# Feed-forward up projections by Strassen's scheme, hidden rows through DRAM, in a two-block kernel

## The chip, the cores and the metric

The kernel runs on one core of a Trainium2 chip. A core has TensorE (PE, matrix products), VectorE (DVE), ScalarE (ACT), GpSimd (POOL), and SyncE (SP), whose queue issues the DMAs. The metric is device time in microseconds (us) of one execution; the median of three runs is given.

## The reference, cut to what matters

Two blocks follow each other on x of 1024 tokens by 1024 features (float32). Each ends its layer with a feed-forward part on a normalised h; the first has 4096 hidden features, the second 2816 of them, made from 2 times 2816 columns through a depthwise convolution over tokens (3 taps).

```python
# first block
h = rmsnorm(x, g_ffn[i])
x = x + jnp.square(jax.nn.relu(h @ w_ffn_up[i])) @ w_ffn_down[i]
...
# second block
h = rms_norm(x, g_ffn[l])
up = depthwise_conv(h @ w_up[l], conv_f_w[l], conv_f_b[l], FFN_CONV // 2)
act = jax.nn.gelu(up[..., :D_FF_2], approximate=True) * up[..., D_FF_2:]
x = x + act @ w_down[l]
```

## The kernel before

Every product is made of three matmuls of a 128x128 weight by 128x512 operand, since each operand is kept as a high and a low part: high by high (L89), high by low (L90), low by high (L91), in `mm3`. `split` (L58, L59) makes the two parts: ScalarE casts the high one, VectorE subtracts it for the low one. `load_w` brings 512 KB of weights in one DMA (`wraw`) and splits them into `whi` and `wlo`, 128x1024 each.

Activations stand transposed, features on partitions, tokens along the row, in two halves of 512 tokens: h0 (high `h0h`, low `h0l`) and h1. An up tile f (128 hidden features) takes, for each half, 8 parts of the inner dimension by 3 matmuls: 48 matmuls and one load of weights. The results are evacuated from PSUM and split into `hh` and `hl` in a ring of 5 pairs (pool "hid"). First feed-forward (`phase_ffn1`): ScalarE relu (L1098), VectorE square (L1099), split. Second (`phase_ffn2`): tiles f and f+22 belong together; each goes through ScalarE (L1487) and two scalar_tensor_tensor on VectorE (L1488, L1489, the outer taps), then gelu (L1495, ScalarE), product (L1496, VectorE), split.

Up and down are interleaved: `ffn` makes the tiles of one group (4, at the start fewer) and one more, then `tm` multiplies the group by its rows of the down weights for all tokens, and `add_x` (L1046, VectorE) adds each PSUM tile into the resident `xres`. A framework sets one static order for each engine and places the waits on semaphores. Before the feed-forward, `norm_rest` starts the up products on the first half of the tokens while the second half is still normalised and transposed (L232, `tr`, TensorE). There are 8 tiles of 128 tokens; `nst` holds their norms, whose small steps are on GpSimd (L194, L196).

Of the kernel before, what the change touches and what calls it, by code (L numbers as in the profile page):

```python
# [27 lines left out]
class Kern:  # L28
# [1035 lines left out]
    def ffn(self, st, nf, up, w_down, last=2, gain=None):  # L1064

        dp = self.pool(st, "hid")
        hid = {}
# [18 lines left out]
        self.behind = ()  # L1086

    def phase_ffn1(self):
        nc, A = self.nc, self.A
        with ExitStack() as st:  # L1090
            self.pp = self.pool(st, "psD", space=PSUM)
            self.mmb = 3
            h = self.norm_rest()

            def up(f, hi, lo):
                def ev(_, ps):
# [483 lines left out]
```

## Time and profile before

| | |
|---|---|
| runs, median (lowest to highest) | 3458.9 us (3456.75 to 3462.65) |
| the profiled execution | 3458.02 us, of which the span of the profile is 3456.0 |
| TensorE busy | 3363.2 us, 97% of the span |
| VectorE, ScalarE, GpSimd busy | 1642.6, 1193.1, 262.6 us |
| mean granted clock of TensorE | 0.994 of full speed |

Busy time is the share of the span in which an engine has an instruction in work. A matmul's busy time overlaps that of the next one (each is shown as about 0.39 us long), so how fast TensorE goes is read from the distance of two starts. The first feed-forward lies at about 1113 to 1790 us and the second at about 2700 to 3456 us of the span.

### The profile page before, as it was taken

The numbers are of one execution on the slowest core, as the hardware profiler recorded it, in microseconds if no ns is written. First come the engines' busy times: TensorE is split into PE (matmuls) and PEld (weight loads), VectorE is DVE, ScalarE is ACT, GpSimd is POOL, SyncE is SP. The second block draws the span as 40 slices with busy tenths as digits, with TensorE's granted clock in tenths as the row PEclk, the third lists the DMA queues.
The fourth block names the chain that finished last, engine by engine and source line by source line (L and its number), as shares of the span: only waits on it lengthen the run. The fifth ranks groups of instructions, "written<-read, shape, count | busy, mean of one in ns | idle before, by whom it ended". The sixth has DMA issues, their size and how long they took to land.

```text
span 3456.0 us, 45568 instructions
## 1 busy us (share of the span) xinstructions
PE 3363.2 (97%) x18990; PEld 2769.9 (80%) x18990; DVE 1642.6 (48%) x2475; ACT 1193.1 (35%) x1624; POOL 262.6 (8%) x448
## 2 busy tenths in 40 slices
PE   8999999999989999999999999999999999999998
PEld 8867777777778888888889977778779888888887
DVE  4445666466554333333343566756343543434434
ACT  4343443477422211111122476652121321211212
POOL 0101111122100000000001411110000000000000
PEclk9999999999999999999999999999999999999999
DMA  3532232332371111111112212222553111211211
GB/s 119 170 107 72 75 78 63 92 85 71 124 274 50 37 49 49 49 49 49 49 55 68 89 56 73 69 75 73 159 188 122 51 49 31 62 48 37 61 49 55
DMA packets 332395, 274.80 MB, mean 80 GB/s; under 512 B 85934, under 2 KB 278814, under 8 KB 332190
## 3 DMA queue, kind: packets, MB, share of 16 engines
q1 hardware_dynamic: 332190, 271.90, 25.6%
q8 instruction: 149, 2.44, 0.3%
q14 instruction: 56, 0.46, 0.0%
HBM read 209.97 MB, written 61.88 MB: 79 GB/s over the span
## 4 chain that ended last, share of the span: by engine, by line
PE 83%; DVE 8%; ACT 5%; issue 2%; DMA 1%; POOL 1%; SPq 0%; DVEq 0%; ACTq 0%; POOLq 0%
PE mm L90 24%; PE mm L89 24%; PE mm L91 24%; PE rps L797 1%; PE tr L232 1%; PE lr L89 1%; PE tp L501 1%; PE rps L713 1%; DVE sq L1301 1%; PE lr L90 1%; DVE hs L1315 1%; PE lr L91 1%; DVE th L1318 1%; DVE ri L1313 1%; DVE wlo L59 1%
## 5 line engine op out<-in xcount | busy, mean ns | idle before, releaser
L58 ACT CAST whi<-wraw 128x1024 fp32r<-128x1024 f32 (+4 forms) x272 | 273.6, 1008 | 1229.7 <-PE mm L90 641.4
L59 DVE TENSOR_TENSOR wlo<-wraw,whi 128x1024 fp32r<-128x1024 f32 (+4 forms) x272 | 318.8, 1176 | 733.8 <-ACT whi L58 728.5
L89 PE MATMUL mm<-h0h,whi 128*128 128x512 f32 x1040 | 405.0, 391 | 6.2 <-ACT h0h L58 2.3
L91 PE MATMUL mm<-h0h,wlo 128*128 128x512 f32 x1040 | 405.6, 390 | 0.0
L90 PE MATMUL mm<-h0l,whi 128*128 128x512 f32 x1040 | 405.1, 390 | 0.1
L90 PE MATMUL mm<-h1l,whi 128*128 128x512 f32 x944 | 368.0, 390 | 0.0
L91 PE MATMUL mm<-h1h,wlo 128*128 128x512 f32 x944 | 367.7, 389 | 0.0
L89 PE MATMUL mm<-h1h,whi 128*128 128x512 f32 x944 | 367.3, 390 | 0.0
L89 PE MATMUL mm<-whi,hh 128*128 128x512 f32 x864 | 339.3, 393 | 1.0 <-DVE cv L1489 0.7
L90 PE MATMUL mm<-wlo,hh 128*128 128x512 f32 x864 | 340.3, 394 | 0.0
L91 PE MATMUL mm<-whi,hl 128*128 128x512 f32 x864 | 335.2, 389 | 0.0
L1046 DVE TENSOR_TENSOR xres<-mm,xres 128x512 f32<-128x512 f32 (+1 forms) x272 | 166.2, 654 | 311.4 <-PE mm L91 311.4
L89 PEld LDWEIGHTS mm<-h0h,whi 128*128 128x128 f32 x1040 | 195.3, 188 | 48.8 <-ACT h0h L58 3.1
L90 PEld LDWEIGHTS mm<-h0l,whi 128*128 128x128 f32 x1040 | 195.5, 188 | 41.2 <-DVE h0l L59 0.6
L91 PEld LDWEIGHTS mm<-h0h,wlo 128*128 128x128 f32 x1040 | 195.6, 188 | 40.8
L89 PEld LDWEIGHTS mm<-h1h,whi 128*128 128x128 f32 x944 | 177.0, 188 | 37.8 <-ACT h1h L58 0.7
L90 PEld LDWEIGHTS mm<-h1l,whi 128*128 128x128 f32 x944 | 177.3, 188 | 37.0
L91 PEld LDWEIGHTS mm<-h1h,wlo 128*128 128x128 f32 x944 | 177.1, 188 | 37.0
L89 PEld LDWEIGHTS mm<-whi,hh 128*128 128x128 f32 x864 | 162.2, 188 | 39.8 <-issue 1.2
L91 PEld LDWEIGHTS mm<-whi,hl 128*128 128x128 f32 x864 | 162.2, 188 | 36.3 <-DVE hl L59 0.3
L90 PEld LDWEIGHTS mm<-wlo,hh 128*128 128x128 f32 x864 | 162.4, 188 | 32.4
L194 POOL TENSOR_SCALAR nst<-nst 128x2 f32<-128x2 f32 (+1 forms) x41 | 10.0, 243 | 2079.1 <-ACT hn L212 1352.8
(477 smaller groups left out, 6357.6 us busy)
## 6 DMA issues: line engine op xcount, KB each, us to landing
wraw<-in_w_in_dram SPq DMA_DIRECT2D x66, 512.0 KB
wraw<-in_w_up_dram SPq DMA_DIRECT2D x44, 512.0 KB
wraw<-in_w_ffn_up_dram SPq DMA_DIRECT2D x32, 512.0 KB
wraw<-in_w_ffn_down_dram SPq DMA_DIRECT2D x32, 512.0 KB
g<-gate_d SPq DMA_DIRECT2D x24, 512.0 KB
wraw<-in_w_down_dram SPq DMA_DIRECT2D x22, 512.0 KB
gate_d<-zg SPq DMA_DIRECT2D x32, 256.0 KB
wraw<-in_w_out_dram SPq DMA_DIRECT2D x16, 512.0 KB
```

The costliest lines, as they stand in the source:

```text
L58: return (self.nc.scalar.copy(out=hi, in_=src), self.nc.vector.tensor_tensor(out=lo, in0=src, in1=hi.bitcast(F32), op=ALU.subtract))
L59: self.nc.vector.tensor_tensor(out=lo, in0=src, in1=hi.bitcast(F32), op=ALU.subtract))
L89: mm(ps, lhsT=sh, rhs=mh, start=first, stop=False)
L90: mm(ps, lhsT=sh, rhs=ml, start=False, stop=False)
L91: mm(ps, lhsT=sl, rhs=mh, start=False, stop=last)
L232: nc.tensor.transpose(ps[:, (k * n + i) * P:(k * n + i + 1) * P], hs[i][:, (k0 + k) * P:(k0 + k + 1) * P], self.ident)
L501: nc.tensor.transpose(tp[:, j * P:(j + 1) * P], pr[:, (j0 + j) * P:(j0 + j + 1) * P], self.ident)
L713: mm(v[R[c], i], lhsT=lhs[R[h], K[i][c]], rhs=ar[R[h], :, K[i][c]], start=True, stop=True)
L797: mm(q4(ps)[:, i], lhsT=lhs[:, 4 * h + i], rhs=rhs[:, i], start=True, stop=True)
L1046: self.nc.vector.tensor_tensor(out=o, in0=ps[:, i], in1=o, op=ALU.add)
L1301: tt(out=sq, in0=r, in1=r, op=ALU.mult)
L1313: tt(out=i, in0=i, in1=th, op=ALU.mult)
```

## The change

**Products.** Both up projections take pairs of up tiles: in the first tiles 2j and 2j+1 (16 pairs), in the second f and f+22 (22 pairs). The inner dimension is cut into two halves of 512, the tokens into two halves of 512, so each pair is a 2 by 2 product of blocks, made by a variant of Strassen's scheme with 7 products, each 4 parts by 3 matmuls of 128x512: 84 matmuls for 96. The token sides are the blocks 11, 21 (the two inner halves of h0), 22, and differences T1, T2, T3, T4 of blocks; 22 and T1 use h1's tiles. They are built once, at the start of each feed-forward, by `t_unit` (four times: 8 transposes, 7 instructions on VectorE, 5 on ScalarE, 1 on GpSimd) and `t_last` (T4). The weight sides are a11, a12, a22 (loaded) and sums `s`, which GpSimd makes for each pair with four instructions of 128x512; three splits of 128x1024 and one of 128x512 (`a22h`, `a22l`) follow. Of the 7 results in PSUM (`p`, six banks), two go through ScalarE and five into additions on VectorE; two more additions of each pair run on GpSimd.

**Way of the hidden rows.** The results are no longer kept: after relu and square (one instruction on VectorE for each 128x512), or convolution, gelu and product, they are written to `hid_d` in DRAM. The down phase follows when all pairs are done: `fetch` loads a row block (`hraw`) and splits it. The first group's down weights are loaded and split ahead (`pre`). T4 and the sums stand where `xres` stood: x is written to `xs_d` in DRAM at the start and read back for the down phase.

**Side of SBUF.** A pool "pad" of 64 bytes a partition moves what follows it on the left side.

The core of the diff (`norm_fm` is only cut in two, and not shown):

```diff
+        self.pool(st, "pad").tile([P, 16], F32, name="pad")
...
+        b12, b22 = ps
+        d = (slice(None), slice(k0, k0 + 2), t)
+        o = {n: [x[d] for x in B[n]] for n in ("11", "22", "T1", "T2", "T3")}
+        f = lambda x: x.bitcast(F32)
+        v = lambda x: x.rearrange("p (k t) -> p k t", k=2)
+        f3 = v(self.tf3[:, k0 * 256:k0 * 256 + HALF])
+        f1 = v(self.sp.tile([P, HALF], F32, tag="tf", name="tf", bufs=2))
+        sub = lambda e, out, a, b: e.tensor_tensor(out=out, in0=a, in1=b, op=ALU.subtract)
+        nc.scalar.copy(out=f3, in_=b12)
+        sub(nc.vector, f1, b12, f(o["11"][0]))
+        sub(nc.vector, f1, f1, f(o["11"][1]))
+        nc.scalar.copy(out=o["22"][0], in_=b22)
+        nc.scalar.copy(out=o["T1"][0], in_=f1)
+        sub(nc.vector, f3, b22, f3)
+        sub(nc.vector, o["22"][1], b22, f(o["22"][0]))
+        sub(nc.vector, o["T1"][1], f1, f(o["T1"][0]))
+        nc.scalar.copy(out=o["T3"][0], in_=f3)
+        sub(nc.gpsimd, o["T3"][1], f3, f(o["T3"][0]))
+        sub(nc.vector, f1, b22, f1)
+        nc.scalar.copy(out=o["T2"][0], in_=f1)
+        sub(nc.vector, o["T2"][1], f1, f(o["T2"][0]))
...
+        tt = (nc.gpsimd if k0 else nc.vector).tensor_tensor
+        tt(out=a, in0=f(b21[0]), in1=f(t2[0]), op=ALU.subtract)
+        tt(out=a, in0=a, in1=f(t2[1]), op=ALU.subtract)
+        tt(out=a, in0=a, in1=f(b21[1]), op=ALU.add)
+        yield
+        nc.scalar.copy(out=t4[0], in_=a)
+        tt(out=t4[1], in0=a, in1=f(t4[0]), op=ALU.subtract)
...
+        def prep(j, i):
+            tt = nc.gpsimd.tensor_tensor
+            if i == 0:
+                split(j, 0, raws[j, 0])
+                return
+            a11, a12 = (raws[j, 0][:, c:c + HALF] for c in (0, HALF))
+            a21, a22 = (raws[j, 1][:, c:c + HALF] for c in (0, HALF))
+            if i == 1:
+                s = ws["s"] = self.sx.tile([P, WCH], F32, tag="s", name="s", bufs=1)
+                tt(out=s[:, :HALF], in0=a21, in1=a22, op=ALU.add)
+                tt(out=s[:, HALF:], in0=s[:, :HALF], in1=a11, op=ALU.subtract)
+                split(j, 1, s)
+            elif i == 2:
+                s = ws["s"]
+                tt(out=s[:, :HALF], in0=a11, in1=a21, op=ALU.subtract)
+                tt(out=s[:, HALF:], in0=a12, in1=s[:, HALF:], op=ALU.subtract)
+                split(j, 2, s)
+            else:
+                split(j, 3, a22)
...
+        def product(j, i, q, b):
+            ps = self.pp.tile([P, HALF], F32, tag="p", name="p", bufs=6)
+            (wh, wl), (bh, bl) = ws[j, i], self.B[b]
+            for k in range(4):
+                self.mm3(ps, wh[:, q, k], wl[:, q, k], bh[:, k], bl[:, k], k == 0, k == 3)
+            return ps
...
+        def consume(j, i):
+            if i == 0:
+                r = r1[j] = tmp(self.sx, "r2", 1) if npre > 2 and j % 3 == 2 else tmp(sp, "r", 2)
+                nc.scalar.copy(out=r, in_=product(j, 0, 0, "11"))
+                outs.append((j, "11", add(V, product(j, 0, 1, "21"), r)))
+            elif i == 1:
+                add(V, product(j, 1, 1, "T2"), r1[j])(r1[j])
+                r5[j] = tmp(sp, "tf", 2)
+                nc.scalar.copy(out=r5[j], in_=product(j, 1, 0, "T1"))
+            elif i == 2:
+                u2 = r1.pop(j)
+                u3 = r1[j] = tmp(sp, "tf", 2)
+                add(V, product(j, 2, 0, "T3"), u2)(u3)
+                add(G, u2, r5[j])(u2)
+                make(j, "22", add(G, u3, r5.pop(j)))
+                make(j, "12", add(V, product(j, 2, 1, "22"), u2))
+            else:
+                make(j, "21", add(V, product(j, 3, 0, "T4"), r1.pop(j)))
+            while outs and self.sx:
+                make(*outs.pop(0))
...
+        self.tf3 = self.gp.tile([P, S], F32, tag="gain1024", name="tf3", bufs=self.gb)
+        hs = self.norm_rows(src, D, gain, (4, 5))
+        self.t_unit(hs, 4, 0)
+        consume(*seq[0])
+        hs2 = self.norm_rows(src, D, gain, (6, 7))
+        self.xst.close()
+        self.sx = self.pool(st, "sx", side="right")
+        B["T4"] = [self.sx.tile([P, 4, HALF], F32R, name="T4" + c) for c in "hl"]
+        self.t_unit(hs, 4, 2)
+        consume(*seq[1])
+        self.t_unit(hs2, 6, 0)
+        loads(npre)
+        prep(*items[npre])
+        self.t_unit(hs2, 6, 2)
+        for q in range(2, npre):
+            consume(*seq[q])
...
+        q = npre
+        for j, i in seq[npre:]:
+            if i < 3:
+                loads(q + 3)
+                if q + 2 < len(items):
+                    prep(*items[q + 2])
+                q += 1
+            if i == 2:
+                prep(j, 3)
+            consume(j, i)
+            if rest and j == 0:
+                next(rest[1 if i == 1 else 3])
+                if i == 1:
+                    next(rest[3])
+                else:
+                    rest = None
...
+        self.hid_d = self.dr.tile([nf * P, S], F32, name="hid_d")
+        self.xs_d = self.dr.tile([S, D], F32, name="xs_d")
+        with ExitStack() as su:
+            self.pp = self.pool(su, "psU", space=PSUM)
+            sp = self.pool(su, "sp")
+            self.strassen(su, w_up, pairs, sp, make, npre)
+        self.pp = self.pool(st, "psD", space=PSUM)
+        self.mmb = 3
...
+        def fetch(f):
+            raw = self.tmp4.tile([P, S], F32, tag="t4", name="hraw")
+            nc.sync.dma_start(out=raw, in_=self.hid_d[f * P:(f + 1) * P, :])
             hid[f] = [dp.tile([P, S], F32R, tag="h" + c, name="h" + c, bufs=5) for c in "hl"]
-            up(f, *hid[f])
-        make(0)
-        self.behind = self.done[0]
+            self.split(*hid[f], raw)
+        cols = [(0, 512), (512, 512)]
+        n = nf % 4 or 4
+        pre = self.load_chunks(w_down, 0, n, cols)
+        for f in range(n):
+            fetch(f)
+        xp = self.pool(self.xst, "x", side="right")
+        self.x = [xp.tile([P, D], F32, name=f"xres{i}") for i in range(NT)]
+        for i in range(NT):
+            nc.sync.dma_start(out=self.x[i], in_=self.xs_d[i * P:(i + 1) * P, :])
         f0 = 0
         while f0 < nf:
             n = (nf - f0) % 4 or 4
-            for f in range(f0 + 1, min(f0 + n + 1, nf)):
-                make(f)
+            for f in range(max(f0 + 1, len(hid)), min(f0 + n + 1, nf)):
+                fetch(f)
             x = lambda k, hf: [t[:, hf * HALF:(hf + 1) * HALF] for t in hid[f0 + k]]
-            if f0 + n < nf:
-                self.tm(x, w_down, f0 * P, n, [[(0, 512), (512, 512)]], self.add_x, per=2)
-            else:
-                self.tm(x, w_down, f0 * P, n, [[(0, 512), (512, 512)]], self.add_x, per=last,
-                        done=None if gain is None else self.norm_first(gain))
+            end = f0 + n >= nf
+            self.tm(x, w_down, f0 * P, n, [cols], self.add_x, per=last if end else 2, pre=pre,
+                    done=self.norm_first(gain) if end and gain is not None else None)
+            pre = None
             f0 += n
...
+                f, hf = 2 * j + int(n[0]) - 1, int(n[1]) - 1
+                o = self.sx.tile([P, HALF], F32, tag="o", name="o", bufs=3)
+                c(o)
+                nc.vector.scalar_tensor_tensor(out=o, in0=o, scalar=0.0, in1=o, op0=ALU.max, op1=ALU.mult)
+                nc.sync.dma_start(out=self.hid_d[f * P:(f + 1) * P, hf * HALF:(hf + 1) * HALF], in_=o)
+            self.ffn(st, 32, A["w_ffn_up"][0], [(2 * j, 2 * j + 1) for j in range(16)], make,
+                     A["w_ffn_down"][0], gain=A["g_ple"][0])
...
+                if n == "12":
+                    g = us[j, 2] = conv(j, us.pop((j, 0)))
+                    nc.scalar.activation(out=g, in_=g, func=AF.Gelu_apprx_tanh)
+                elif n == "21":
+                    g = us.pop((j, 2))
+                    c2 = conv(j + NF, us.pop((j, 1)))
+                    nc.vector.tensor_tensor(out=g, in0=g, in1=c2, op=ALU.mult)
+                    nc.sync.dma_start(out=self.hid_d[j * P:(j + 1) * P, :], in_=g)
+            self.ffn(st, NF, A["w_up_2"][0], [(j, j + NF) for j in range(NF)], make, A["w_down_2"][0], last=1, npre=2)
```

**What stands in a row, VectorE where the first feed-forward begins.** Before, from the last two additions into `xres` (`h1l` is the low part of a piece of h1, the two `hn` are the normalised last two token tiles):

```order
L1046 TENSOR_TENSOR xres_10237<-mm,xres_10237 128x512 [waits PE_49]
L1046 TENSOR_TENSOR xres_10238<-mm,xres_10238 128x512
L59 TENSOR_TENSOR h1l<-tr,h1h 128x2x256 [waits Activation_49] x2
L59 TENSOR_TENSOR wlo<-wraw,whi 128x1024 [waits DMAHW3_49,Activation_49]
L216 SCALAR_TENSOR_TENSOR hn<-xres_10237,nst,gain 128x1024 [waits Activation_49,Pool_49]
L216 SCALAR_TENSOR_TENSOR hn<-xres_10238,nst,gain 128x1024 [waits Activation_49]
L59 TENSOR_TENSOR h1l<-tr,h1h 128x2x256 [waits Activation_49] x6
L59 TENSOR_TENSOR wlo<-wraw,whi 128x1024 [waits DMAHW4_49,PE_49,Activation_49]
L1099 TENSOR_TENSOR r<-r 128x1024 [waits Activation_49]
L59 TENSOR_TENSOR hl<-r,hh 128x1024 [waits Activation_49]
L59 TENSOR_TENSOR wlo<-wraw,whi 128x1024 [waits DMAHW5_49,PE_49,Activation_49]
L1099 TENSOR_TENSOR r<-r 128x1024 [waits Activation_49]
```

Now, from the same two additions (whose line is L1052 there; L1097 is `t_unit`, L1122 `t_last`, `tf` are float32 differences of blocks, L1180 an addition of a product `p`, L1328 relu and square):

```order
L1052 TENSOR_TENSOR xres_10241<-mm,xres_10241 128x512 [waits PE_49]
L1052 TENSOR_TENSOR xres_10242<-mm,xres_10242 128x512
L1097 TENSOR_TENSOR tf<-tr,h0h 128x512 [waits Activation_49]
L1097 TENSOR_TENSOR tf_11027<-tr,tf_11027 128x512 [waits Activation_49]
L1097 TENSOR_TENSOR tf<-tf,h0l 128x512 [waits DVE_49]
L1097 TENSOR_TENSOR h1l<-tr,h1h 128x2x256
L215 SCALAR_TENSOR_TENSOR hn<-xres_10241,nst,gain 128x1024 [waits Activation_49,Pool_49]
L1097 TENSOR_TENSOR h1l<-tf,h1h 128x2x256 [waits Activation_49]
L215 SCALAR_TENSOR_TENSOR hn<-xres_10242,nst,gain 128x1024
L1097 TENSOR_TENSOR tf<-tr,tf 128x512 [waits DVE_49]
L1180 TENSOR_TENSOR o<-p,r 128x512 [waits DMAHW6_49,PE_49,Activation_49]
L1097 TENSOR_TENSOR tf<-tr,h0h 128x512 [waits Activation_49]
```

and it goes on in this manner up to these, of which the last is the last low part of T2:

```order
L1328 SCALAR_TENSOR_TENSOR o<-o 128x512 [waits DVE_49]
L1097 TENSOR_TENSOR tf<-tr,tf 128x512 [waits DVE_49]
L1122 TENSOR_TENSOR tf_11027<-h0h,T2h 128x512 [waits Pool_49]
L59 TENSOR_TENSOR wlo<-s,whi 128x1024
L1097 TENSOR_TENSOR T2l<-tf,T2h 128x2x256 [waits Activation_49]
```

From the first of the two additions to that last T2l there are now 41 instructions: 2 `hn` and 2 `wlo` of 128x1024, and 37 of 128x512. On TensorE, 98 matmuls stand between the last matmul of the phase before and the one that needs it. In the second feed-forward it is 39 instructions (35 of 128x512) and 74 matmuls.

**VectorE, end of the up phase of the second feed-forward.** Before, the first group of the down projection (the hidden tiles of the first two pairs) follows the products of the third pair. What VectorE has in a row there, from the low part of the second pair's hidden tile:

```order
L59 TENSOR_TENSOR hl<-cv,hh 128x1024 [waits Activation_49]
L59 TENSOR_TENSOR wlo<-wraw,whi 128x1024 [waits DMAHW4_49,PE_49,Activation_49]
L1488 SCALAR_TENSOR_TENSOR cv<-mm,vcol_conv_f_b,cv 128x1023 [waits Activation_49]
L1489 SCALAR_TENSOR_TENSOR cv<-mm,vcol_cw_364,cv 128x1023 [waits DVE_49]
L59 TENSOR_TENSOR wlo<-wraw,whi 128x1024 [waits DMAHW5_49,PE_49,Activation_49]
L1488 SCALAR_TENSOR_TENSOR cv<-mm,vcol_conv_f_b,cv 128x1023 [waits Activation_49]
L1046 TENSOR_TENSOR xres_20936<-mm,xres_20936 128x512 [waits PE_49]
L1489 SCALAR_TENSOR_TENSOR cv<-mm,vcol_cw_364,cv 128x1023 [waits DVE_49]
L1046 TENSOR_TENSOR xres_20937<-mm,xres_20937 128x512
L1496 TENSOR_TENSOR cv<-cv 128x1024 [waits DVE_49]
```

Now, from the addition of the very last product up to the first two low parts that the down phase needs:

```order
L1180 TENSOR_TENSOR u_25483<-p,tf 128x512 [waits DMAHW1_49,PE_49]
L1712 SCALAR_TENSOR_TENSOR cv<-u,vcol_cw_368,cv 128x1023 [waits DVE_49]
L1711 SCALAR_TENSOR_TENSOR cv<-u_25483,vcol_conv_f_b,cv 128x1023 [waits Activation_49]
L1712 SCALAR_TENSOR_TENSOR cv<-u_25483,vcol_cw_368,cv 128x1023 [waits DVE_49]
L1728 TENSOR_TENSOR cv<-cv 128x1024 [waits DVE_49,Activation_49]
L59 TENSOR_TENSOR hl<-hraw,hh 128x1024 [waits DMAHW1_49,Activation_49]
L59 TENSOR_TENSOR hl<-hraw,hh 128x1024 [waits DMAHW4_49,Activation_49]
L1052 TENSOR_TENSOR xres_25560<-mm,xres_25560 128x512 [waits DMAHW2_49,PE_49]
```

TensorE there, before and now, from the last matmul of an up product:

```order
L91 MATMUL mm<-h1h,wlo 128x512
L89 MATMUL mm<-whi,hh 128x512 [waits DVE_49,Activation_49]
L90 MATMUL mm<-wlo,hh 128x512
L91 MATMUL mm<-whi,hl 128x512
L89 MATMUL mm<-whi,hh 128x512 [waits Activation_49]
L90 MATMUL mm<-wlo,hh 128x512
L91 MATMUL mm<-whi,hl 128x512 [waits DVE_49]
```

```order
L91 MATMUL p<-T4h,a22l 128x512
L89 MATMUL mm<-whi,hh 128x512 [waits DVE_49,Activation_49]
L90 MATMUL mm<-wlo,hh 128x512
L89 MATMUL mm<-whi,hh 128x512
L90 MATMUL mm<-wlo,hh 128x512
L91 MATMUL mm<-whi,hl 128x512 [waits DVE_49]
```

Before, both `hl` of the first group stood ahead of the evacuation of the third pair. The first `hl` of the down phase now stands on VectorE behind all the evacuation of the last up tile, and TensorE has four matmuls that need no `hl` ahead of the first that does. In the first feed-forward the same place has two VectorE instructions (addition, L1328) and then five `hl`, and TensorE six matmuls ahead of the first on `hl`.

## Rows read from the trace of the kernel before

**Rows 1.** The page of the kernel before: span, busy time, chain that ended last.
```profile
span 3456.0 us, 45568 instructions
...
PE 3363.2 (97%) x18990; PEld 2769.9 (80%) x18990; DVE 1642.6 (48%) x2475; ACT 1193.1 (35%) x1624; POOL 262.6 (8%) x448
...
PE 83%; DVE 8%; ACT 5%; issue 2%; DMA 1%; POOL 1%; SPq 0%; DVEq 0%; ACTq 0%; POOLq 0%
```

**Rows 2.** Stretches: busy us by engine (x instructions), granted clock, DMA share, GB/s.
```profile
1150.00:1780.00 630.00, 630.00 (x2767) 519.25 (x2766) 209.98 (x230) 120.11 (x118) 0.00 (x0) 1.00 0.17 49
2760.00:3380.00 620.00, 620.00 (x2728) 511.95 (x2727) 261.38 (x253) 142.79 (x134) 0.00 (x0) 1.00 0.16 49
960.00:970.00 10.00, 0.52 (x3) 0.08 (x1) 0.69 (x1) 0.00 (x0) 0.00 (x0) 0.63 0.81 258
970.00:980.00 10.00, 4.80 (x11) 3.36 (x12) 6.05 (x5) 5.83 (x6) 0.00 (x0) 0.52 0.88 312
980.00:990.00 10.00, 10.00 (x46) 8.23 (x45) 7.12 (x7) 4.75 (x7) 0.00 (x0) 1.00 0.85 300
```

**Rows 3.** TensorE's waits, 2760 to 3456 us: for whom, us in total, times, longest.
```profile
PE mm L89 <- DVE cv L1489: 0.7, 1, 0.7
PE mm L89 <- DVE xres L1046: 0.3, 1, 0.3
```

**Rows 4.** TensorE's timeline in the first feed-forward: start, length, instruction.
```profile
1305.15 0.39 PE L89 MATMUL mm<-h0h,whi 128*128 128x512 f32 x1
...
1339.15 0.39 PE L89 MATMUL mm<-h0h,whi 128*128 128x512 f32 x1
```

**Rows 5.** TensorE's timeline where the first feed-forward begins.
```profile
1113.64 1.04 PE L232 MATMUL tr<-ident,hn 128*128 128x128 f32 x8
1116.20 0.47 PE L89 MATMUL mm<-h0h,whi 128*128 128x512 f32 x1 [1.52 <-DVE xres L1046]
```

**Rows 6.** VectorE's timeline at the same place.
```profile
1114.77 1.28 DVE L1046 TENSOR_TENSOR xres<-mm,xres 128x512 f32<-128x512 f32 x2
...
1120.40 2.48 DVE L216 SCALAR_TENSOR_TENSOR hn<-xres,nst,gain 128x1024 f32<-128x1024 f32 x2 [1.92 <-POOL nst L196]
```

**Rows 7.** VectorE's groups by shape, 1090 to 1790 us, then 2690 to 3456 us.
```profile
L59 DVE TENSOR_TENSOR wlo<-wraw,whi 128x1024 fp32r<-128x1024 f32 x64 | 78.2, 1224 | 247.8 <-ACT whi L58 247.8
...
L59 DVE TENSOR_TENSOR h1l<-tr,h1h 128x512 fp32r<-128x512 f32 x8 | 5.3, 688 | 7.3 <-ACT h1h L58 7.3
...
L1489 DVE SCALAR_TENSOR_TENSOR cv<-mm,vcol_cw,cv 128x1023 f32<-128x1023 f32 x44 | 56.4, 1283 | 1.5
...
L1496 DVE TENSOR_TENSOR cv<-cv 128x1024 f32<-128x1024 f32 x22 | 26.9, 1225 | 0.7
```

**Rows 8.** GpSimd's timeline, 509 to 513 us.
```profile
509.69 1.28 POOL L686 TENSOR_TENSOR ar<-e 128x512 f32<-128x512 f32 x1
...
511.06 1.79 POOL L772 TENSOR_TENSOR l<-amb,low 128x512 f32<-128x512 f32 x1
```

**Rows 9.** GpSimd's timeline, 1895 to 1899 us, then 1943 to 1950 us.
```profile
1895.98 1.43 POOL L1151 TENSOR_TENSOR xres<-xres,sg 128x256 f32<-128x256 f32 x2 [3.55 <-DVE sg L1148]
...
1945.08 3.39 POOL L1151 TENSOR_TENSOR xres<-xres,sg 128x256 f32<-128x256 f32 x2
```

**Rows 10.** VectorE's timeline, 1944 to 1950 us.
```profile
1944.64 1.55 DVE L59 TENSOR_TENSOR wlo<-wraw,whi 128x1024 fp32r<-128x1024 f32 x1
1946.12 1.76 DVE L1193 SCALAR_TENSOR_TENSOR hn<-xres,nst,gain 128x1024 f32<-128x1024 f32 x1
1947.80 1.75 DVE L59 TENSOR_TENSOR wlo<-wraw,whi 128x1024 fp32r<-128x1024 f32 x1
```

**Rows 11.** ScalarE's group of the convolution's middle tap, 2690 to 3456 us.
```profile
L1487 ACT ACTIVATE cv<-mm,vcol_conv_f_b,vcol_cw 128x1024 f32<-128x1024 f32 x44 | 53.0, 1205 | 0.0
```

**Rows 12.** One load of weights: issue on SyncE's queue, then its cast on ScalarE.
```profile
1300.86 0.37 SPq L78 DMA_DIRECT2D wraw<-in_w_ffn_up_dram  x1
...
1305.96 1.05 ACT L58 CAST whi<-wraw 128x1024 fp32r<-128x1024 f32 x1 [0.89 <-DMA wraw<-in_w_ffn_up_dram]
```

More of the change, by code (lines that the diff above doesn't have):

```diff
@@ L1062, in norm_rest, with t_unit @@
         return h
-    def ffn(self, st, nf, up, w_down, last=2, gain=None):
+    def t_unit(self, hs, t0, k0):
+        nc, B = self.nc, self.B
+        tt = nc.vector.tensor_tensor
+        t = slice((t0 % 4) * P, (t0 % 4 + 2) * P)
+        ps = []
+        for kk in (k0, k0 + 4):
+            q = self.tpp.tile([P, HALF], F32, tag="tp", name="tr", bufs=2)
+            for k in range(2):
+                for i in range(2):
+                    nc.tensor.transpose(q[:, (k * 2 + i) * P:(k * 2 + i + 1) * P],
+                                        hs[i][:, (kk + k) * P:(kk + k + 1) * P], self.ident)
+            ps.append(q.rearrange("p (k t) -> p k t", k=2))
+        b12, b22 = ps
[19 more added lines that the diff above has]
+        sub(nc.vector, o["T2"][1], f1, f(o["T2"][0]))
@@ L1066, in ffn @@
+    def ffn(self, st, nf, w_up, pairs, make, w_down, last=2, gain=None, npre=3):
+        nc = self.nc
+        self.hid_d = self.dr.tile([nf * P, S], F32, name="hid_d")
[6 more added lines that the diff above has]
+        self.mmb = 3
         dp = self.pool(st, "hid")
@@ L1090, in phase_ffn1, with make @@
         with ExitStack() as st:
[L1091 to L1096, printed above, removed]
-                    r = self.tmp4.tile([P, S], F32, tag="t4", name="r")
-                    nc.scalar.activation(out=r, in_=ps, func=AF.Relu)
-                    nc.vector.tensor_tensor(out=r, in0=r, in1=r, op=ALU.mult)
-                    self.split(hi, lo, r)
-                self.fm(h, A["w_ffn_up"][0], 8, f * P, 1, ev)
-            self.ffn(st, 32, up, A["w_ffn_down"][0], gain=A["g_ple"][0])
+            def make(j, n, c):
+                f, hf = 2 * j + int(n[0]) - 1, int(n[1]) - 1
[5 more added lines that the diff above has]
+                     A["w_ffn_down"][0], gain=A["g_ple"][0])
     def phase_ple(self):
@@ L1474, in phase_ffn2 @@
         with ExitStack() as st:
[L1475 to L1477 removed]
+            us = {}
             stt = nc.vector.scalar_tensor_tensor
[L1480 to L1497 removed]
@@ L1498, in phase_ffn2, with conv @@
-            self.ffn(st, NF, up, A["w_down_2"][0], last=1)
+            def conv(f, u):
+                one = lambda nm: v[nm][:, f:f + 1]
+                c = self.tmp4.tile([P, S], F32, tag="t4", name="cv")
+                nc.scalar.activation(out=c, in_=u, func=AF.Identity, scale=one("cw1"), bias=one("conv_f_b"))
+                stt(out=c[:, 1:], in0=u[:, :S - 1], scalar=one("cw0"), in1=c[:, 1:], op0=ALU.mult, op1=ALU.add)
+                stt(out=c[:, :S - 1], in0=u[:, 1:], scalar=one("cw2"), in1=c[:, :S - 1], op0=ALU.mult, op1=ALU.add)
+                return c
@@ new lines, in make @@
+            def make(j, n, c):
+                r, hf = int(n[0]) - 1, int(n[1]) - 1
+                if n == "11":
+                    us[j, 0] = self.sx.tile([P, S], F32, tag="o", name="u", bufs=2)
+                elif n == "22":
+                    us[j, 1] = self.tmp4.tile([P, S], F32, tag="t4", name="u2")
+                c(us[j, r][:, hf * HALF:(hf + 1) * HALF])
+                if n == "12":
[6 more added lines that the diff above has]
+                    nc.sync.dma_start(out=self.hid_d[j * P:(j + 1) * P, :], in_=g)
```

116 lines of the change are left out of this document (82 added, 34 removed).

## The prediction

> **What bounds the kernel now.** The page first [rows 1]: TensorE is busy for 97% of the span and makes 83% of the chain that ended last; no other engine comes to half. Then two stretches inside the feed-forwards [rows 2]: in 630 and 620 us TensorE is busy for all of it at full clock, while VectorE has work for 210 and 261 us, ScalarE for 120 and 143, GpSimd for none, and DMA moves 49 GB/s. The list of waits bears it out: in the second feed-forward TensorE waits for 1.0 us in all [rows 3], at the start of the first once for 1.52 us [rows 5]. Both are bound by the number of matmuls, and each one that goes gives back its slot as long as nothing else becomes late. The slot is read from starts, since busy times overlap: the 150th matmul after the one at 1305.15 starts at 1339.15 [rows 4], so 34.00/150 = 0.2267 us.
>
> **What is removed.** A pair of up tiles took 2 x 48 = 96 matmuls and takes 84. With 16 and 22 pairs that is 38 x 12 = 456 matmuls, 456 x 0.2267 = **103.4 us**. One pair now lasts 84 x 0.2267 = 19.04 us on TensorE, and all that is added must fit beside that.
>
> **What is added in each pair, and its cover.** VectorE, by its groups [rows 7]: three low parts of weights at 1.22, one at 0.69, five additions from PSUM at 0.69 (the nearest row of that width), together 7.8. The first feed-forward adds four of L1328 at 0.69: 10.6. The second adds four convolution steps at 1.28 and a product at 1.23: 14.2. GpSimd: six instructions of 128x512 at 1.28 [rows 8], 7.7. ScalarE: at most nine instructions in a pair, none longer than the 1.21 of the convolution's middle tap [rows 11], so under 10.9. DMA: two loads of 512 KB and up to two stores of as much are 2.1 MB, 110 GB/s over 19.04 us, where the trace shows 300 and more [rows 2]. Each is below 19.04, so TensorE stays the bound in the body and these cost nothing. The tightest is the second feed-forward's VectorE with GpSimd, a rival below. In the down phase a group of 192 matmuls (43.5 us) has eight transfers of 512 KB, 96 GB/s. x is read back when T4's space is free; its first load takes some 5 us as a weight load does from issue to use (1300.86 to 1305.96) [rows 12], and TensorE can go on into three PSUM tiles (8.2 us in the second feed-forward, 16.3 in the first) before it needs the first addition. I cost this at nothing, too. The pad moves addresses only: nothing.
>
> **A lock between VectorE and GpSimd.** Two GpSimd instructions (L1151) take 1.43 alone and 3.39 in another place [rows 9]; in that place three VectorE instructions with two SBUF inputs take 1.55, 1.76, 1.75 [rows 10], where such take 1.22 to 1.28 undisturbed [rows 7]: 5.06 for 3.72. The excess of 1.34 is about GpSimd's own 1.43, so the two don't run together but take turns. One 128x512 of GpSimd likewise took 1.79 for 1.28 [rows 8]. So where VectorE is the bound, GpSimd's time falls partly on it.
>
> **The starts.** This is the largest cost. Call T0 the end of the matmuls before; the second half's tokens come in after it. VectorE starts its last two additions into x at T0 + 1.13 (1113.64 to 1114.77) [rows 5, 6]. From there to the last T2l it has, in the first feed-forward, 37 instructions of 128x512 and 4 of 128x1024. Two of the former in a row take 1.28 [rows 6], 0.64 each: 37 x 0.64 + 4 x 1.23 = 28.6, so T0 + 29.7 without a wait. About 14.6 of it has two SBUF inputs, and GpSimd has eight instructions there (four T3l, four sums), 10.2 us; if they collide in proportion (14.6/28.6) VectorE loses 5: T0 + 34.7. I take that also to stand for its waits on norms, of which one of 1.92 is seen [rows 6]; bounds are 0 and the whole 10.2. TensorE has 98 matmuls (22.2) and 32 transposes (4 x 1.04) [rows 5] ahead of the matmul that needs it: 26.4. Idle 8.3, of which 1.5 was there before: **6.8**. Second feed-forward: 35 x 0.64 + 4.9 + 1.1 + 5 = 33.4 against 74 matmuls and the transposes, 21.0: **12.4**, and none before. T4 follows from T2l by three GpSimd steps, a cast and two sums in the way, 7.0 to 7.5, against 22 to 30 matmuls (5.0 to 6.8): **2** for both, bounds 0 and 6.
>
> **Up to down.** Before, up tiles covered each split of a hidden tile; now the first ones stand behind the last evacuation. First feed-forward: matmul end 0.2, addition 0.64, L1328 0.64, `hl` 1.22 make 2.7 after the last product, and TensorE has 6 matmuls (1.4) that need no `hl`; three more `hl` at 1.22 against 4 or 5 matmuls each cost some tenths: **2**. Second: 0.2 + 0.64 + three convolution steps at 1.28 + product 1.23 + `hl` 1.22 = 7.1 against 4 matmuls (0.9): **6**. ScalarE's steps lie beside these. Bounds 5 and 11 for both (a wait behind a weight split, or a lock, more or less).
>
> **Between groups of the down phase.** With a ring of 5 pairs, three of the next four tiles can be split only when the last tokens of a group are done: 3 x 1.22 = 3.66 against 16 matmuls (3.63). 7 + 5 boundaries; I take 0.3 each, **3.6**, bounds 0 and 2.5 each (two VectorE instructions late).
>
> **Sum.** Costs 6.8 + 12.4 + 2 + 8 + 3.6 = 32.8. Against the profiled execution's 3458.0 (span 3456.0 and 2.0 around it; 0.9 under the median of the runs): 3458.0 - 103.4 + 32.8 = **3387 us**. All low bounds (no lock 1.8 + 7.4, T4 0, 5, 0: 14) give 3369, no cost at all 3355; all high bounds (12 + 17.6 + 6 + 11 + 30 = 77) 3431.
>
> **Rivals.**
> *VectorE and GpSimd in turns bind the second feed-forward.* If every GpSimd instruction shut VectorE out, a pair would take 14.2 + 7.7 = 21.8 for 19.04: 22 x 2.8 = 61 more, 3448; with half of that 3418. For it the stretched instructions [rows 8 to 10]. Against it: only 10.7 of the 14.2 have two SBUF inputs, and VectorE still has 4.8 us of a pair idle, in which GpSimd can run; six PSUM banks give 13.6 us of slack. In the first feed-forward the same sum, 10.6 + 7.7 = 18.3, stays below the pair. The Trainium skill (SBUF — State Buffer, "Who interferes with whom") says that GpSimd shares one pair of VectorE's ports, locked for whole instructions, and that a VectorE instruction with at most one SBUF input doesn't contend. By that rule a pair has 10.7 + 7.7 = 18.4 of exclusive work, TensorE stays the bound, and the sum stays at 3387. The trace agrees on two inputs (5.06 for 3.72); no row here shows the other half. Chance 0.17.
>
> *Slower: the preparation of weights becomes the bound.* For each pair a load (5.1) [rows 12], two sums (2.6), a cast (1.05), a low part (1.22), and two more sums into the same single buffer `s` (2.6) follow one another, 12.5 of 19.04; VectorE and GpSimd take them in order between additions that wait for products, so that a late product makes late weights. It decides from 70.6/38 = 1.86 us a pair, at 20.9 us the gain is gone; at 22 the time is 3387 + 38 x 2.96 = 3500. For it: a third of slack is not much for a chain through four engines. Against it: weights stand almost a pair ahead. Chance 0.07.
>
> *The clock falls at the starts.* TensorE was busy for 0.52 us of 960 to 970 and got 0.52 of full clock in the next ten, then full clock again [rows 2]. Idle pieces at a start add to 12 us at most, between matmuls; if they do it, each start loses some 5: 3397. Chance 0.05.
>
> **Chances.** My forecast 0.68 (alone 3362 to 3425), the lock 0.17 (3395 to 3449), the slow rival 0.07, the clock 0.05, less cost than the low bounds 0.03. What a measurement can tell from no change is 0.2%, 7 us. Faster by more: 0.92; within: 0.02; slower: 0.06. The range 3362 to 3430 holds the forecast, the clock and over half of the lock; its low end leaves only the second start's 7 us.
>
> **What would show it.** A body of 84 matmuls at 0.2267 without waits in both feed-forwards (right); two idle stretches of TensorE behind T2l of about 8 and 12 us, and one of 6 before the second down phase (the costs); waits of TensorE for `wlo<-s` or for PSUM banks that come back in each pair would show a rival, as would GpSimd's mean well above 1.28 with VectorE busy throughout. I am wrong if such waits repeat in pairs, or if the starts cost tens of us.

## The result

Four runs of the changed kernel gave a median of **3476.56 us** (3476.41 to 3482.99), beside 3457.82 (3456.27 to 3462.65) for the kernel before: ratio 1.0057, 95% interval 1.0045 to 1.0069. The kernel is 0.6% slower where 2% faster was forecast. The profiled execution is the highest of the four, 3482.99 (its span 3481.3). Of what it takes over the profile of before, 7.7 us lie ahead of the first feed-forward (its first product starts at 1123.87 for 1116.20), in code that the change leaves alone; there the granted clock was lower in some stretches (0.87 for 0.96 at 320 to 360 us).

The page of the changed kernel, the lines that answer to [rows 1]:

```profile
span 3481.3 us, 46328 instructions
...
PE 3297.0 (95%) x18534; PEld 2696.5 (77%) x18534; DVE 1896.1 (54%) x2829; ACT 1272.3 (37%) x1776; POOL 599.4 (17%) x700
...
PE 61%; DVE 14%; POOL 8%; ACT 6%; issue 6%; DMA 5%; SPq 0%; POOLq 0%; DVEq 0%; ACTq 0%
```

TensorE has less to do, 3297.0 us for 3363.2, and less of the chain that ended last is its own: 61% for 83%. VectorE, GpSimd, waits for DMA and "issue" have taken its place.

TensorE's timeline of the changed kernel (start, length, instruction, idle before it and who ended it), at the first product of the first feed-forward, its first matmul on T4 and its first down matmul, then the same three of the second:

```profile
1123.87 0.47 PE L89 MATMUL p<-h0h,whi 128*128 128x512 f32 x1 [1.55 <-DVE xres L1052]
...
1179.62 0.79 PE L89 MATMUL p<-T4h,a22h 128*128 128x512 f32 x1 [13.21 <-ACT T4h L1126]
...
1466.28 0.47 PE L89 MATMUL mm<-whi,hh 128*128 128x512 f32 x1 [3.46 <-DVE o L1180]
...
2720.84 0.48 PE L89 MATMUL p<-h0h,whi 128*128 128x512 f32 x1
...
2766.90 0.79 PE L89 MATMUL p<-T4h,a22h 128*128 128x512 f32 x1 [6.00 <-ACT T4h L1126]
...
3228.85 0.79 PE L89 MATMUL mm<-whi,hh 128*128 128x512 f32 x1 [12.07 <-ACT hh L58]
```

The up phases, from the first product to the first down matmul, take 342.4 and 508.0 us. Their matmuls alone would take 1344 x 0.2267 = 304.7 and 1848 x 0.2267 = 418.9. So 38 and 89 us go to other things, 3 of each to the 24 transposes that lie inside; beside the transposes the forecast had some 11 and 20. From first product to last down matmul, the first feed-forward went from 706.5 to 698.8 us, the second from 725.1 to 752.3.

Three kinds of place lose it, as stretches show (columns as in [rows 2], the engines in the order PE, PEld, DVE, ACT, POOL; PEld is TensorE's loading of weights):

```profile
1160.00:1180.00 20.00, 6.79 (x23) 5.15 (x22) 13.49 (x13) 3.85 (x5) 17.30 (x12) 0.67 0.18 52
1180.00:1200.00 20.00, 17.93 (x68) 14.05 (x68) 9.59 (x11) 5.20 (x6) 8.88 (x8) 0.81 0.53 171
1240.00:1260.00 20.00, 20.00 (x90) 16.56 (x89) 10.16 (x14) 4.93 (x7) 7.60 (x6) 1.00 0.34 110
2980.00:3000.00 20.00, 18.26 (x78) 13.99 (x77) 11.86 (x14) 7.91 (x9) 7.57 (x6) 1.00 0.24 78
3220.00:3240.00 20.00, 10.79 (x34) 8.21 (x35) 13.46 (x14) 5.57 (x5) 1.92 (x2) 0.66 0.88 311
```

The body of the first feed-forward is as forecast: TensorE is busy for all of 1240 to 1260, and the pairs there are 19.04 us apart (two late ones 19.11 and 19.47). Its start is not: 6.79 of 20 us busy at 0.67 of full clock, with GpSimd busy for 17.30. The body of the second feed-forward has 78 matmuls in 20 us for 90. And where its down phase begins TensorE is busy for 10.79 of 20.

**The body of the second feed-forward.** Who waited for whom, all engines, 2860 to 3200 us, about 15.5 pairs (us in total, times, longest):

```profile
POOL s L1166 <- DVE wlo L59: 163.2, 16, 10.2
...
DVE u L1180 <- POOL r L1180: 75.2, 15, 5.4
POOL s L1161 <- DMA wraw<-in_w_up_dram: 60.5, 15, 4.5
...
PEld p L89 <- DVE u L1180: 38.8, 31, 2.2
```

Each wait occurs once in each pair, the last one twice. That is how a loop looks: no engine is busy throughout (VectorE 11.86 of 20 us, GpSimd 7.57), and all wait for one another. The chain that ended last, in order of time, shows one turn of it (start, length, what):

```profile
3002.16 1.29 POOL s L1166
3003.46 1.26 POOL s L1167
3004.73 3.94 DMA wraw<-in_w_up_dram
3008.80 1.29 POOL s L1161
3010.17 1.29 POOL s L1162
3011.46 1.24 POOL r L1180
...
3013.34 1.48 DVE wlo L59
3014.92 1.27 DVE cv L1711
3016.20 0.61 DVE u L1180
...
3022.75 1.23 DVE wlo L59
3024.12 1.29 POOL s L1166
```

The second sums (L1166, L1167) release a raw weight buffer; only then is the next pair's weight loaded into it (3.94); the next first sums follow (L1161, L1162); behind them in GpSimd's queue stand the pair's additions (L1180), whose last operand VectorE had finished at 3007.7 (its timeline has that addition at 3006.97, 0.68 long); VectorE waits for these, and its evacuation stands in a row up to the low part of the first sums (3022.75), for which the next second sums wait, since both sums use the one tile `s`. From 3002.16 to 3024.12 it is 21.96 us; TensorE needs 19.04.

**The start of the first feed-forward.** GpSimd's timeline there:

```profile
1151.71 1.59 POOL L1097 TENSOR_TENSOR T3l<-tf,T3h 128x512 fp32r<-128x512 f32 x1 [3.37 <-ACT T3h L1106]
...
1159.65 1.56 POOL L1127 TENSOR_TENSOR T4l<-tf,T4h 128x512 fp32r<-128x512 f32 x1 [0.73 <-ACT T4h L1126]
1161.18 1.72 POOL L1161 TENSOR_TENSOR s<-wraw 128x512 f32<-128x512 f32 x1
1162.87 1.74 POOL L1122 TENSOR_TENSOR tf<-h0h,T2h 128x512 f32<-128x512 f32 x1
1164.57 1.28 POOL L1162 TENSOR_TENSOR s<-s,wraw 128x512 f32<-128x512 f32 x1
...
1167.16 2.14 POOL L1124 TENSOR_TENSOR tf<-tf,h0l 128x512 f32<-128x512 f32 x1
...
1174.14 1.26 POOL L1180 TENSOR_TENSOR r<-r,tf 128x512 f32<-128x512 f32 x1
```

GpSimd's queue is full: from 1151.71 to 1176.6 it makes the last T3l, eight instructions of T4, four sums of the second pair and two additions, nine of the fifteen stretched from 1.28 to between 1.5 and 2.1 us. TensorE waits 13.21 us for T4 (timeline above). The part of T4 that comes last is not one of GpSimd's own but the last of VectorE's, and it is late through GpSimd all the same: in VectorE's queue it stands behind an addition, and that one waits 3.60 us for the first of GpSimd's two additions (`r`, 1174.14). VectorE's timeline:

```profile
1175.44 0.69 DVE L1180 TENSOR_TENSOR o<-p,r 128x512 f32<-128x512 f32 x1 [3.60 <-POOL r L1180]
1176.05 1.13 DVE L1123 TENSOR_TENSOR tf<-tf,T2l 128x512 f32<-128x512 f32 x1
...
1178.23 0.68 DVE L1124 TENSOR_TENSOR tf<-tf,h0l 128x512 f32<-128x512 f32 x1
```

ScalarE casts this into T4h, and TensorE goes on at 1179.62. It comes back at half of full clock: the granted 0.50 is 1.20 GHz of 2.40.

```profile
1170.00:1175.00 5.00, 0.00 (x0) 0.00 (x0) 1.84 (x2) 0.79 (x1) 4.97 (x4) 0.54 0.00 0
1175.00:1180.00 5.00, 0.38 (x1) 0.39 (x2) 4.56 (x5) 0.88 (x2) 3.10 (x3) 0.50 0.35 105
1180.00:1185.00 5.00, 2.93 (x7) 1.82 (x7) 4.04 (x4) 1.05 (x1) 2.51 (x3) 0.50 0.46 151
```

### The profile page after: what moved, and what is told of

Its sections match the earlier page's. It is cut to its first block, busy times and chain, and to the rows that moved or that the text cites. A ratio compares the mean times of both kernels' runs of the same rounds, so it can differ in the third digit from the quotient of the medians.

```text
span 3481.3 us, 46328 instructions
## 1 busy us (share of the span) xinstructions
PE 3297.0 (95%) x18534; PEld 2696.5 (77%) x18534; DVE 1896.1 (54%) x2829; ACT 1272.3 (37%) x1776; POOL 599.4 (17%) x700
## 4 chain that ended last, share of the span: by engine, by line
PE 61%; DVE 14%; POOL 8%; ACT 6%; issue 6%; DMA 5%; SPq 0%; POOLq 0%; DVEq 0%; ACTq 0%
PE mm L89 16%; PE mm L90 16%; PE mm L91 16%; DVE wlo L59 3%; DMA wraw<-in_w_up_dram 2%; DMA wraw<-in_w_ffn_up_dram 1%; POOL s L1166 1%; POOL s L1167 1%; POOL r L1180 1%; PE p L89 1%; POOL s L1161 1%; PE rps L803 1%; PE p L90 1%; PE p L91 1%; DVE cv L1711 1%
## 5 line engine op out<-in xcount | busy, mean ns | idle before, releaser
L58 ACT CAST whi<-wraw 128x1024 fp32r<-128x1024 f32 (+3 forms) x234 | 232.3, 1001 | 796.9 <-PE mm L91 456.3
L59 DVE TENSOR_TENSOR wlo<-wraw,whi 128x1024 fp32r<-128x1024 f32 (+3 forms) x234 | 279.7, 1203 | 260.7 <-ACT whi L58 255.7
L89 PE MATMUL mm<-whi,hh 128*128 128x512 f32 x864 | 338.1, 393 | 17.2 <-ACT hh L58 12.1
L91 PE MATMUL mm<-whi,hl 128*128 128x512 f32 x864 | 336.6, 391 | 0.4 <-DVE hl L59 0.4
L1052 DVE TENSOR_TENSOR xres<-mm,xres 128x512 f32<-128x512 f32 (+1 forms) x272 | 166.4, 653 | 306.4 <-PE mm L91 305.1
L89 PEld LDWEIGHTS mm<-whi,hh 128*128 128x128 f32 x864 | 162.8, 189 | 55.4 <-ACT hh L58 12.5
L89 PE MATMUL mm<-h0h,whi 128*128 128x512 f32 x432 | 167.9, 392 | 3.8 <-ACT h0h L58 1.4
L91 PE MATMUL mm<-h0h,wlo 128*128 128x512 f32 x432 | 169.1, 391 | 0.0
L90 PE MATMUL mm<-h0l,whi 128*128 128x512 f32 x432 | 168.8, 391 | 0.1
L91 PE MATMUL mm<-h1h,wlo 128*128 128x512 f32 x336 | 131.0, 390 | 0.0
L90 PE MATMUL mm<-h1l,whi 128*128 128x512 f32 x336 | 131.0, 390 | 0.0
L89 PE MATMUL mm<-h1h,whi 128*128 128x512 f32 x336 | 130.7, 390 | 0.0
L89 PE MATMUL p<-h1h,whi 128*128 128x512 f32 x304 | 121.0, 398 | 6.0 <-DVE u L1180 6.0
L90 PE MATMUL p<-h1l,whi 128*128 128x512 f32 x304 | 119.3, 392 | 0.0
```

The lines of the kernel that those rows point to most:

```text
L58: return (self.nc.scalar.copy(out=hi, in_=src), self.nc.vector.tensor_tensor(out=lo, in0=src, in1=hi.bitcast(F32), op=ALU.subtract))
L59: self.nc.vector.tensor_tensor(out=lo, in0=src, in1=hi.bitcast(F32), op=ALU.subtract))
L89: mm(ps, lhsT=sh, rhs=mh, start=first, stop=False)
L90: mm(ps, lhsT=sh, rhs=ml, start=False, stop=False)
L91: mm(ps, lhsT=sl, rhs=mh, start=False, stop=last)
L1052: self.nc.vector.tensor_tensor(out=o, in0=ps[:, i], in1=o, op=ALU.add)
```

## The experiments

Each was timed against the kernel before on the same chip, four or five runs; the changed kernel's own ratio is 1.0057 (1.0045 to 1.0069). Where two intervals overlap, a difference of their medians shows nothing by itself, and the profiles are read beside it.

**1. GpSimd's additions ahead of the next first sums.**

```diff
-                tt(out=s[:, :HALF], in0=a21, in1=a22, op=ALU.add)
+                with ExitStack() as es:
+                    if "g" in ws:
+                        es.enter_context(self.tc.issue_after(ws["g"].ins))
+                    tt(out=s[:, :HALF], in0=a21, in1=a22, op=ALU.add)
...
                 loads(q + 3)
+                if i == 2:
+                    prep(j, 3)
+                    consume(j, i)
                 if q + 2 < len(items):
                     prep(*items[q + 2])
                 q += 1
-            if i == 2:
-                prep(j, 3)
-            consume(j, i)
+            if i != 2:
+                consume(j, i)
```

(`ws["g"]` is the second addition.) The edit moves more than the two additions: the split of a22 and VectorE's two additions of the same step now stand ahead of the next sums, too.

> GpSimd's two additions of a pair are issued ahead of the two first sums of the next pair; nothing else is changed. Theory of the loop: in the second feed-forward a pair takes 21.85 us because second sums (2.6) release a raw weight buffer, its load takes 4.1, the next first sums take 2.6, the additions stand behind them (1.3), and VectorE's row from there to the low part of the first sums takes 11.3, on which the second sums wait. Without the additions behind the load a pair goes to TensorE's 19.05, some 20 pairs x 2.8 = 55 less: about 3422 (3415 to 3435). Theory of the lock (VectorE and GpSimd in turns, 14.2 + 7.7 = 21.8): the same work is done, so the pair stays at 21.8 and the time at 3477.

3471.72, ratio 1.0038 (1.0023 to 1.0053): far from the 55 us expected. What there is of a gain lies in the first feed-forward, whose up phase fell from 342.4 to 336.6 us; in the second it took 508.8 for 508.0. The chain that ended last shows why:

```profile
3012.67 1.29 POOL u L1183
3013.97 1.26 POOL s L1164
...
3015.29 1.30 POOL s L1165
3016.61 1.06 ACT whi L58
3017.69 1.24 DVE wlo L59
...
3019.00 2.27 POOL s L1169
3021.27 2.25 POOL s L1170
3023.54 1.05 ACT whi L58
3024.62 1.18 DVE wlo L59
...
3034.30 1.29 POOL u L1183
```

The load is out of the loop, and another one has closed there, 21.63 us long (3012.67 to 3034.30): additions, first sums, their cast and low part, second sums, again cast and low part, VectorE's evacuation, additions. It, too, goes through `s`: the second sums begin only when the low part of the first is done. The expectation had removed one edge and not looked for the next longest loop. Some 2 us of this turn come from VectorE and GpSimd taking turns: the two second sums take 2.27 and 2.25 where the first ones take 1.26 and 1.30, beside a convolution step on VectorE (its timeline):

```profile
3020.64 1.72 DVE L1718 SCALAR_TENSOR_TENSOR cv<-u,vcol_cw,cv 128x1023 f32<-128x1023 f32 x1
```

So without that this turn would be, by estimate, 21.63 - 1.94 = 19.7 us, still above 19.04.

**2. A tile of their own for the second sums, second feed-forward.**

```diff
-                s = ws["s"]
-                tt(out=s[:, :HALF], in0=a11, in1=a21, op=ALU.subtract)
-                tt(out=s[:, HALF:], in0=a12, in1=s[:, HALF:], op=ALU.subtract)
-                split(j, 2, s)
+                s, s2 = ws["s"], ws["s"]
+                if npre == 2:
+                    s2 = self.sx.tile([P, WCH], F32, tag="s2", name="s2", bufs=1)
+                tt(out=s2[:, :HALF], in0=a11, in1=a21, op=ALU.subtract)
+                tt(out=s2[:, HALF:], in0=a12, in1=s[:, HALF:], op=ALU.subtract)
+                split(j, 2, s2)
...
-                    us[j, 0] = self.sx.tile([P, S], F32, tag="o", name="u", bufs=2)
+                    us[j, 0] = self.sx.tile([P, S], F32, tag="o", name="u", bufs=1)
```

> Second feed-forward only: the second sums are written to a tile of their own and so wait no longer for the low part of the first sums (the space comes from one of the two buffers u). Theory of the loop: it is cut at this edge; the additions then stand behind four sums, so a pair takes 19.05 to 20: 3425 to 3445. Theory of the lock: no change, 3477.

3433.44, ratio 0.9928 (0.9911 to 0.9944), 43 us less than the changed kernel. A stretch of the body:

```profile
2900.00:3000.00 100.00, 100.00 (x442) 82.82 (x442) 73.00 (x74) 41.14 (x46) 47.52 (x35) 1.00 0.25 79
```

TensorE is busy for all of it, and from the third pair on all are 19.04 us apart, with the same instructions on VectorE and GpSimd as before the edit. So the loop through `s` was the bound of this body. The lock alone was not, although the prediction's price for it, 21.8 us a pair, is by chance the measured one.

**3. Control: one u buffer, sums as in the change.** (The last two lines of the diff above alone.)

> Control of the tile for the second sums, which had its space from one of two buffers u: here one u buffer alone, the sums as in the change. Theory of the loop: no gain, 3474 to 3480. If it was the buffer u that made the order or a wait better: a good part of the 43 us, below 3460.

3476.73, ratio 1.0046 (1.0029 to 1.0063): the gain is that of the tile.

**4. T4 on VectorE alone.**

```diff
-        tt = (nc.gpsimd if k0 else nc.vector).tensor_tensor
+        tt = nc.vector.tensor_tensor
```

> All of T4 is made on VectorE (before: half of it on GpSimd, eight instructions of 1.3 to 2.1 us in each start). Theory that GpSimd's own queue is late at the starts (it was busy for 17.3 of the 20 us ahead of T4): the wait of 13.2 us for T4 in the first and 6.0 in the second feed-forward fall by more than half together, with some clock: 3460 to 3468. Theory that VectorE is the bound there, as the prediction had it: eight instructions more on VectorE at 0.6 to 1.2 make each start 5 to 8 longer: 3486 to 3492.

3469.51, ratio 1.0032 (1.0019 to 1.0045): 7 us less, just outside the 3460 to 3468 of the first expectation, and far from the second. The wait for T4 in the first feed-forward is nearly gone (TensorE's waits, 1110 to 1200 us):

```profile
PE p L90 <- DVE T4l L1127: 2.5, 2, 1.7
...
PE p L89 <- ACT T4h L1126: 0.6, 1, 0.6
```

T4h costs 0.6 for 13.2 us. What the eight instructions cost on VectorE is small (T4l 2.5 for 2.1). The body of the first feed-forward is slower now: eleven of its pairs take 19.4 to 21.2 us, 7.5 us more in all. The chain that ended last runs there through second sums, load, first sums and additions, too: the first feed-forward has the loop of the second, only shorter. The first up phase fell from 342.4 to 333.5 us, the second only from 508.0 to 507.2: while the loop set the pace there, an earlier T4 was of no use.

**5. Edits 2 and 4 together.**

> The second sums in a tile of their own in the second feed-forward, and all of T4 on VectorE. If the loop over `s` hid what T4 on VectorE gave in the second start (there the up phase took 508.0 and 507.2 us with T4 half on GpSimd and all on VectorE), then with the loop cut both starts give: 9 in the first, about 9 of the 11.8 us that TensorE waited for T4 in the second: 3433.4 - 18 = 3415 (3410 to 3422). If GpSimd's queue was late only in the first feed-forward: 3424 to 3426.

3412.78, ratio **0.9864** (0.9850 to 0.9879), as expected of two causes that had hidden one another in the second start. This version beats both kernels: 1.4% faster than the one before.

**6. T4 left out, on the kernel of experiment 2.** (`t_last`, which makes T4, is emptied as well.)

```diff
-                make(j, "21", add(V, product(j, 3, 0, "T4"), r1.pop(j)))
+                make(j, "21", add(V, product(j, 3, 0, "T3"), r1.pop(j)))
```

> On the kernel with the second sums in their own tile (3433.4): T4 is not built, and the products with T4 are taken with T3 (this part of the computation is changed), the number of matmuls is the same. Theory that T4, late in GpSimd's queue, and the clock that falls behind its wait make most of what the starts cost: the waits of 16.0 and 11.8 us go, with some 5 us of clock in each: 3395 to 3405. Theory that VectorE's 41 and 39 instructions to the last T2l make it, with T4 a small end: they remain, and no more than 12 us go: 3421 or more.

3408.64 (ratio 0.9852, 0.9838 to 0.9867), 25 us less than experiment 2, a little above the range of the first theory: T4 with the clock behind it was 11 us in the first up phase (341.7 to 331.0) and 16 in the second (464.4 to 448.5). The 11 are net: as in experiment 4, the pairs that follow are slower than 19.04. What is left of the second start are waits ahead of the last T2l, 2.4 us for T2h and these:

```profile
PE tr L1087 <- DVE tf L1097: 12.4, 4, 4.5
```

**7. GpSimd's additions ahead in the first feed-forward, beside edits 2 and 4.** (Edit 1 under the condition `npre > 2`, which holds in the first feed-forward alone.)

> The second sums in their own tile in the second feed-forward, T4 on VectorE, and in the first feed-forward GpSimd's additions ahead of the next pair's sums. In the run with the first two edits (3412.8) the first feed-forward's pairs took 19.55 us by the same loop; in the run with the additions ahead they took 19.04. Theory of the loop: 12 to 14 pairs x 0.5 = 6 to 7 less, 3406 (3402 to 3410). If TensorE's pace there was set by something else: 3412 to 3414.

3414.39 (ratio 0.9867, 0.9851 to 0.9884), not told apart from experiment 5: a miss. In the profile the pairs of the first feed-forward are 19.04 us apart, as expected (in experiment 5 eleven of them take 19.5 to 21.1, 7.7 us more in all), but the other order of issue let TensorE wait 7.4 us for T4 (3.2 in experiment 5), and most of the gain went there: the up phase fell by 3.0 us, 334.4 to 331.4.

**8. a22 where the first tiles of x stood.**

```diff
+        for c in "hl":
+            self.sx.tile([P, HALF], F32R, tag="a22" + c, name="a22" + c)
         B["T4"] = [self.sx.tile([P, 4, HALF], F32R, name="T4" + c) for c in "hl"]
```

> The a22 parts are laid where the first tiles of x stood instead of the last, so that ScalarE's cast of a22 no longer waits 5.3 us for the last spill of x to DRAM in the first start. If that wait, behind which all of ScalarE's casts stand, is on the path: 3 to 6 us less, 3471 to 3474. If the wait for T4 comes last whatever ScalarE does there: no change, 3476 to 3478.

3479.54 (ratio 1.0062, 1.0047 to 1.0077), no gain. The wait for x's spill is gone from the profile, and TensorE still waited 12.0 us for T4: that wait was not the one that ended last.

**9. The new scheme in the first feed-forward alone.**

> The new scheme in the first feed-forward alone; the second is that of the kernel before. From the profiles the first feed-forward gained 7.7 us (706.5 to 698.8 from its first product to its last) and the second lost 27.2: about 3459.7 - 8 = 3452 (3447 to 3455). If the loss is shared between the two in another way (a start that delays what follows), another time.

3446.52 (ratio 0.9960, 0.9945 to 0.9974), 13 us less than the kernel before, somewhat more than the profiles gave (7.7). So, against the kernel before, the whole loss lies in the second feed-forward. Against the forecast the first falls short as well: 16 x 12 x 0.2267 = 43.5 us of matmuls are gone there, the forecast left it some 32 of them, and 13 show.

**10. Without the pad.**

> The change without its pool of 64 bytes. The addresses of the left side of SBUF do nothing to the time, so 3475 to 3479. If the shift mattered (to a DMA or to an engine's reads), a difference of more than 0.2%.

3483.94 (ratio 1.0069, 1.0053 to 1.0084). The median lies outside the expected 3475 to 3479, a miss by 5 us, but the interval overlaps that of the change (1.0045 to 1.0069), so no effect of the 64 bytes is shown; a gain of 0.1% from them, or somewhat more, can't be excluded.

## Why the prediction was wrong

**What failed.** The step "Each is below 19.04, so TensorE stays the bound in the body and these cost nothing". It compared each engine's busy time in a pair with TensorE's and left out the order in which they wait. In the second feed-forward that order closes a loop of 21.9 us through the queues of GpSimd, SyncE and VectorE. The forecast had the loop among its rivals (the slow one, 0.07), but priced it at 12.5 us: load, sums, cast, low part. It missed two edges that stand in the order of issue. The load waits for the second sums of the pair before, as the raw buffers are a ring of three; and GpSimd's additions stand behind the next first sums, with VectorE's whole evacuation (11.3 us) behind them. The rival's mark of 20.9 us a pair was right for both feed-forwards together; here the second slowed down, by some 2.8 us on 16 of its 22 pairs, 47 us in all with the pairs at either end of them. Experiment 2 gave 43 us back; with the loop cut, waits at the start came to show (T4 11.8 us for 6.0, transposes 11.7 for 7.7), and the change to the down phase got shorter. That the first feed-forward stayed at 19.04 is in part luck: where TensorE starts its body earlier (experiments 4 and 5), its loop shows too, with pairs of 19.4 to 21.2. That the late start gave its weights a lead in the change is likely, and not shown.

**The other terms.**
- 103.4 us removed: right. The slot of 0.2267 held, and bodies in which no loop was longer ran at 19.04 a pair (first feed-forward of the change; second in experiment 2).
- Last T2l, 6.8 and 12.4: about right. TensorE's waits ahead of it (transposes, T2, weights) are 7.4 us in the first start; 9.9 in the second, where 14.8 show once the loop is cut and T4 left out.
- T4, 2 us for both: the second mis-sized term. It took 25 us (experiment 6). From the end of the last T2l (1159.47) to the first matmul on T4 (1179.62) it was 20.1 us, for 7.0 to 7.5. GpSimd was weighed as what delays VectorE, and its own queue was not added up: twelve instructions on T3 and T4, eight sums and two additions, many stretched by VectorE; and VectorE's part of T4 waits on that queue through an addition.
- The clock: a rival with 0.05, at 5 us a start. It was part of what happened, and its size was right: 0.50 to 0.54 of full clock in 1170 to 1185, behind the wait for T4, and in the first 100 us of the two up phases 34 and 31 matmuls that start over 0.3 us after the one before without a wait, 6.4 and 6.0 us over slots of 0.2267. With it the first feed-forward's 38 us are nearly found: transposes 3, ahead of the last T2l 7.4, T4 15.3 (T4h 13.2, T4l 2.1), clock 6.4, up to down 3.5.
- Up to down, 2 and 6: 3.5 and 12.1 us were measured. With the loop cut, the second is 6.1 + 0.6 us, as forecast; in the change VectorE came late out of the last turn, and the cast of a row waited 3.2 us for its load from DRAM.
- Between groups 0.3: the stretches of the down phase have 19.82 of 20 us busy where a boundary lies, so 0.2.

**The lock**, as the rival of VectorE and GpSimd in turns is called here, is seen, and it is not what bounded the change. The Trainium skill (SBUF — State Buffer, "Who interferes with whom") says that a VectorE instruction with at most one SBUF input stays clear of GpSimd, which no row of the kernel before showed. VectorE's timeline of the changed kernel, beside GpSimd's rows at 1159.65 to 1164.57 above, agrees:

```profile
1160.00 1.77 DVE L59 TENSOR_TENSOR a22l<-wraw,a22h 128x512 fp32r<-128x512 f32 x1
1161.69 1.77 DVE L1124 TENSOR_TENSOR tf<-tf,h0l 128x512 f32<-128x512 f32 x1
1163.38 0.68 DVE L1180 TENSOR_TENSOR r<-p,r 128x512 f32<-128x512 f32 x1
```

The two with both inputs in SBUF take 1.77 for 0.68; the addition from PSUM (`p`, `r`) takes 0.68 while GpSimd runs. The page's rule gave 18.4 us of exclusive work a pair and TensorE as the bound; the 19.04 us a pair of experiment 2 agree with that. The lock does lengthen a turn where it falls on one: by some 0.4 us in the change (VectorE's `wlo` at 3013.34 takes 1.67 for 1.22 by its timeline), by some 2 in experiment 1.

**Open.** What the starts would cost with other orders of T1 to T3, and whether a tile of its own for the second sums would help the first feed-forward (not tried).
